# Other durations and a shared port in the build-time forecast of a two-layer fp32 backbone

## The chip, the cores and the metric

The kernel runs on one core of one Trainium2 chip. The metric is the time of one execution on the device in microseconds (us), as the median of several runs. In what follows PE is TensorE (and PEld its loading of stationary tiles), DVE is VectorE, ACT is ScalarE, POOL is GpSimd, and SP is SyncE, whose queue issues most transfers.

## The reference, cut to what matters

Two layers work on 512 latent tokens and 256 context tokens of width 1024, in fp32. Each layer has three token mixers side by side (multi-head latent attention, a bidirectional gated linear recurrence, HGRN2, and differential attention), fed by one input projection. Their outputs are merged by gates, and a SwiGLU block follows.

```python
for l in range(DEPTH):                                   # DEPTH = 2
    sh1, sc1, g1, sh2, sc2, g2 = split(silu(c) @ w_mod[l] + b_mod[l], 6)
    y_x, y_c = token_mixer(x * (1 + sc1) + sh1, ctx * (1 + csc1) + csh1, ...)
    x = post_norm(x, g1 * y_x, ln1_g[l], ln1_b[l])
    x = post_norm(x, g2 * swiglu(x * (1 + sc2) + sh2, w_ff1[l], w_ff2[l]), ...)
    # the context stream likewise, in layer 0 only
# token_mixer: y0 = latent attention, y1 = HGRN2, y2 = differential attention
m = sum(sigmoid(h @ w_gate[i] + b_gate[i]) * (y[i] @ w_branch[i]) for i in range(3))
y = m @ w_o
```

## The kernel before

**Products.** A weight block of 128 x 1024 is loaded (wr), cast to a rounded type (wh), and what the cast lost is subtracted out (wl = wr - wh). The activations are split in the same way (h, k, s or ac, in two tiles each). A product is then three matmuls: high by high, high by low, low by high (`mm3`, line 462). The accumulators are PSUM banks of 512 columns, named b; S names the pair of two-bank tiles. Every weight block is a `Job`, and `dstep` (line 394) emits the next few matmuls of the current job: six of them, then it gives its cost by `mmcost`. `do_conv` and `split_w` (lines 365 and 352) make wh and wl a job or two ahead, `pump` (line 332) issues the loads.

**Chains.** The attentions, the recurrence and the layer norms are written as generators of small steps, each of which waits for the one before: `mla`, `diff` and `hgrn` in this order, then the norms. In the recurrence (`hgrn`, line 1334) each of the four heads runs seven levels. A level has the products S of kc and QQ on PE (line 1406), an update of the key tile KK on POOL (line 1411), a copy kc of it by ACT for the next level, two updates of the query tile QQ and a masked copy out of S on DVE (lines 1424 and 1426). KK, QQ and TT are called k in the profile, since all come from one pool; kc, and everything else of one slab, is called s. Behind the last level come transposes of KK, the running states, the output products, a norm, and the store of y to DRAM (line 1503). The last merge reads y back (`yprep`, line 1525), and its eight products with `w_branch` can't begin without it. The eight products with `w_gate` ahead of them can.

**What sets the order.** Nothing does at run time but the five queues and the semaphores. The order within a queue is the order in which the build emits instructions. `weave` (line 433) runs a chain's generator; where the chain says `At(t)`, the time at which its next operands are due, it emits `dstep`s of products until PE's forecast time gets to t - 0.1. The forecast is the class `Clock` (line 110): for each instruction emitted it works out a start (its engine free, operands written, the output tile free) and a duration by engine, operation and columns, in `note` (line 188). Two choices read the forecast as well: `split_w` gives the cast to POOL rather than ACT where POOL is forecast to be over 1 us earlier (not within the recurrence), and `lo_eng` (line 360) gives the subtraction of certain jobs to DVE rather than POOL within the recurrence, where DVE is forecast to be free earlier than POOL plus 1 us. `pump` loads a block when its buffer is forecast to be free within 3 us of PE's time. Every instruction goes through the helper at line 106, so all rows of the profile have that line.

Of the kernel before, what the change touches and what calls it, by code (L numbers as in the profile page):

```python
# [10 lines left out]
F32 = mybir.dt.float32  # L11
# [28 lines left out]
def mmcost(n):  # L40
    return max(n, 250) * 0.000422

# [55 lines left out]
class Port:  # L98
    """an engine's queue, each instruction noted by the clock before it is emitted"""
    def __init__(self, clock, eng):  # L100
# [9 lines left out]
class Clock:  # L110
    """A coarse forecast, in us, of when each engine gets to what is put in its queue and when each tile is written.
    It only decides how many steps of the weight products are put between two steps of a latency-bound chain."""

    def __init__(self, nc):
        self.nc = nc
        self.at = dict(tensor=0.0, vector=0.0, scalar=0.0, gpsimd=0.0, sync=0.0)
        self.busy = []
        self.wrote, self.used, self.prev, self.rings = {}, {}, {}, {}
        for e in ("tensor", "vector", "scalar", "gpsimd", "sync"):
            setattr(self, e, Port(self, e))  # L120

    def ring(self, key, bufs, tile):
        """the tile takes the buffer of the one allocated bufs before it under the same tag"""
        r = self.rings.setdefault(key, [])
        name = tile.tensor.name
        r.append(name)
        if len(r) > bufs:
            self.prev[name] = r[-bufs - 1]
        return tile
# [35 lines left out]
    def next(self, key, bufs):  # L165
        """when a tile allocated now under this tag can be written"""
        r = self.rings.get(key, ())
        return self.whole(r[-bufs]) if len(r) >= bufs else 0.0

    def mark(self, log, ap, end, eng):  # L170
# [5 lines left out]
    def transfer(self, t, c):  # L176
        """the first free stretch of the DMA rings from t on"""
        for i, (a, b) in enumerate(self.busy):
            if a >= t + c:
                self.busy.insert(i, (t, t + c))  # L180
                break
            t = max(t, b)
        else:
            self.busy.append((t, t + c))
        self.busy = self.busy[-100:]
        return t + c

    def note(self, eng, op, a, k):
        outs = [a[0]] + ([k["accum_out"]] if "accum_out" in k else [])
        ins = [x for x in list(a[1:]) + list(k.values()) if hasattr(x, "tensor") and hasattr(x, "ap")]  # L190
        sizes = [x.free_size() for x in outs[:1] + ins]
        n = sizes[0] if eng == "tensor" else max(sizes[:3])
# [7 lines left out]
        if op == "dma_start":  # L200
            self.at[eng] = start + (0.53 if eng == "sync" else 1.1)
            end = self.transfer(start + 0.6, outs[0].size() * 4 / 360e3) + 1.4
        else:
            if eng == "tensor":
                slow = op == "transpose" or n < 250 or ins[0].dtype == F32
                c, lat = max(n * (0.00084 if slow else 0.000422), 0.03) * (2 if ins[0].dtype == F32 and op != "transpose" and n < 250 else 1), 0.2
            elif eng == "vector":
                c, lat = 0.065 + n * (0.00052 if op == "tensor_copy" else 0.00065 if op == "tensor_scalar" else 0.00105), 0.15
            elif eng == "scalar":
                c, lat = 0.09 + n * 0.00083 + (0.1 if len(outs) > 1 else 0.0), 0.15  # L210
            else:
                c = 0.13 + n * (0.00101 if op == "tensor_scalar" else 0.00212) + (0.3 if ALU.pow in a else 0.0)
                lat = 0.15
            self.at[eng] = start + c
# [7 lines left out]
class At:  # L222
    """go on when the products put in the queue reach this time"""
    def __init__(self, t):
# [17 lines left out]
class Kern:  # L242
# [144 lines left out]
    def ahead(self, i, n):  # L387
        """the end of the list of weights up to the n-th after the i-th that goes to the tensor engine"""
        while n and i + 1 < len(self.wjobs):
            i += 1  # L390
            n -= self.wjobs[i].conv is None
        return i + 1
# [106 lines left out]

    # ---------------------------------------------------------------- setup  # L500
    def setup(self):
# [20 lines left out]
    def setup_rows(self):  # L522
        """loads of the small parameters, as rows"""
        nc, I, cp = self.nc, self.I, self.cp
# [85 lines left out]

    # ---------------------------------------------------------------- adaLN modulation vectors
    def mod_block(self, l, blk, direct=False):
# [60 lines left out]
    def mod_block_v(self, l, blk):  # L673
        """as mod_block, the products and their sum over blocks of 128 inputs elementwise, the sum over partitions by ones"""
        nc, I = self.nc, self.I
# [81 lines left out]
    def affine(self, key, l, which, ln):  # L757
        """per-feature gain and offset of x -> x * (1 + sc) + sh, after the gain and offset of a layer norm if any"""
        nc = self.nc
# [12 lines left out]
    def mod_tile(self, key, t, xo, h):  # L772
        """h[:, :, tile t] = transpose(xo) * A + B, split in two parts"""
        hx = self.ln4()
# [33 lines left out]

    # ---------------------------------------------------------------- latent query/key front
    def b1_load(self, l, u, dma):  # L810
# [157 lines left out]

    # ---------------------------------------------------------------- combined input projection (rest)
    def win_jobs(self, l, names):  # L970
        """feature-major tiles of w_in, parked in DRAM"""
        nc = self.nc
# [21 lines left out]

    # ---------------------------------------------------------------- multi-head latent attention
    def mla(self, l):
# [134 lines left out]

    # ---------------------------------------------------------------- differential attention
    def diff(self, l):
# [194 lines left out]

    # ---------------------------------------------------------------- bidirectional gated recurrence
    def vw(self, t, off, dims):  # L1330
# [184 lines left out]

    # ---------------------------------------------------------------- gated merge
    def merge_jobs(self, l, br, seq):
# [66 lines left out]

    # ---------------------------------------------------------------- token-major output products
    def sweep_jobs(self, key, w, nk, tiles, lhs, use_s, needs=(), keep=2):
        """acc[t] = lhs(:, t)^T w; the last blocks of w are kept for a pass tile by tile, so that the tiles end one after the other"""
        nc = self.nc
# [60 lines left out]
    def ln_front(self, x1, r):  # L1649
        """x1 <- ALPHA * r + x1; the scale and offset of its normalization"""  # L1650
        nc = self.nc
# [72 lines left out]

    # ---------------------------------------------------------------- FFN
    def ff1_jobs(self, l):
# [267 lines left out]
```

## Time and profile before

| what | us |
|---|---|
| median of 3 runs | 3069.2 (3064.12 to 3072.55) |
| span of the profiled execution, which is its own time | 3064.3 |
| PE busy, in all | 2825.8 |
| DVE busy | 1628.7 |
| ACT busy | 1137.7 |
| POOL busy | 974.2 |
| layer 0: latent attention, from 172 to 408 | 236 |
| layer 0: differential attention, 408 to 652 | 244 |
| layer 0: recurrence, 652 to 946 | 294 |
| layer 1: the same three, 1899 to 2106, to 2303, to 2546 | 207, 197, 243 |

The span is the time from the first to the last instruction of the one execution that was profiled. Busy times of different engines overlap. A stage here is the stretch in which the chain of that mixer runs, with products of the weights between its steps; I set its ends by the first and last instructions of the chain. "Clock" below is the granted clock of TensorE as a share of 2.4 GHz; at 0.5 it is at its lower level, 1.2 GHz.

### The profile page before, as it was taken

What the parts mean: (1) busy time and instruction counts of PE and PEld (TensorE: products, weight loads), DVE (VectorE), ACT (ScalarE), POOL (GpSimd) and SP (SyncE); (2) the same over time, 40 slices, a digit from 0 to 9 for tenths busy, and PEclk for the clock granted to TensorE, in tenths of its full rate; (3) what the DMA queues carried; (4) which work ended last, traced back from release to release, by engine and by line L of the source; (5) the groups of instructions that cost most, each with busy time, mean ns of one, the idle gap of its engine ahead of it and who ended that gap; (6) DMA issues with size and microseconds to landing.
All of it is one profiled execution on the core that took longest, in us unless ns stands there. A gap on an engine that the chain in (4) does not pass through costs nothing. (4 is left out here: it accounts for less than half of the span.)

```text
span 3064.3 us, 39087 instructions
## 1 busy us (share of the span) xinstructions
PE 2825.8 (92%) x14899; PEld 2346.2 (77%) x14899; DVE 1628.7 (53%) x2413; ACT 1137.7 (37%) x2177; POOL 974.2 (32%) x688
## 2 busy tenths in 40 slices
PE   6999989998799997999999898999998899799997
PEld 3888866677688885888888677887776777688875
DVE  4455566657762038555543665445656762632235
ACT  4544434443332124344332445444444332322222
POOL 1333433334444434243320223333324555300002
PEclk8999999999999998999999999999999999899998
DMA  6423243343333354354443354324223343433331
GB/s 211 129 80 97 91 136 96 100 141 103 101 111 110 103 169 151 117 152 143 119 137 96 110 167 122 89 83 131 79 73 127 104 132 123 146 107 96 103 131 69
DMA packets 345523, 359.14 MB, mean 117 GB/s; under 512 B 31114, under 2 KB 263044, under 8 KB 345336
## 3 DMA queue, kind: packets, MB, share of 16 engines
q1 hardware_dynamic: 343144, 351.84, 37.0%
q10 hardware_dynamic: 1680, 4.42, 0.4%
q8 instruction: 117, 1.92, 0.3%
q14 instruction: 70, 0.57, 0.1%
q0 software_dynamic: 512, 0.39, 0.1%
HBM read 298.10 MB, written 58.49 MB: 116 GB/s over the span
## 5 line engine op out<-in xcount | busy, mean ns | idle before, releaser
L106 PE MATMUL b<-h,wh 128*128 128x512 f32 (+1 forms) x5152 | 1385.0, 358 | 32.2 <-ACT h L106 14.2
L106 PEld LDWEIGHTS b<-h,wh 128*128 128x128 f32 x5152 | 911.5, 193 | 168.3 <-ACT h L106 15.1
L106 PE MATMUL b<-h,wl 128*128 128x512 f32 (+1 forms) x2576 | 909.5, 353 | 0.0
L106 DVE TENSOR_TENSOR wl<-wr,wh 128x1024 fp32r<-128x1024 f32 (+1 forms) x253 | 373.0, 1478 | 458.3 <-ACT wh L106 457.3
L106 PEld LDWEIGHTS b<-h,wl 128*128 128x128 f32 x2576 | 496.6, 193 | 66.4 <-DVE wl L106 0.3
L106 ACT CAST wh<-wr 128x1024 fp32r<-128x1024 f32 (+1 forms) x298 | 295.0, 993 | 415.2 <-PE b L106 331.2
L106 POOL TENSOR_TENSOR sm<-sm,mhalf 128x1 f32<-128x1 f32 (+3 forms) x80 | 56.7, 709 | 1035.7 <-DVE sm L106 1035.7
L106 POOL TENSOR_TENSOR wl<-wr,wh 128x1024 fp32r<-128x1024 f32 (+1 forms) x131 | 285.5, 2179 | 222.4 <-ACT wh L106 199.9
L106 ACT ACTIVATE s<-S,sm 128x768 f32<-128x768 f32 (+1 forms) x170 | 135.2, 796 | 377.7 <-DVE sm L106 325.2
L106 POOL TENSOR_TENSOR ln<-ln,wr 128x512 f32<-128x512 f32 x84 | 119.5, 1423 | 222.9 <-issue 161.6
L106 PE MATMUL S<-wh,ac 128*128 128x512 f32 x512 | 173.8, 404 | 16.4 <-DVE ac L106 11.2
L106 PE MATMUL S<-k,s 128*128 128x128 f32 (+2 forms) x704 | 150.8, 336 | 37.8 <-DVE k L106 33.8
L106 DVE TENSOR_TENSOR k<-b,k 128x512 fp32r<-128x512 f32 (+1 forms) x136 | 85.0, 627 | 175.0 <-ACT k L106 174.7
L106 PE MATMUL S<-k,k 96*128 96x512 f32 (+2 forms) x576 | 153.0, 366 | 22.8 <-DVE k L106 11.8
L106 PE MATMUL b<-k,wh 128*128 128x512 f32 (+1 forms) x576 | 161.5, 368 | 10.5 <-ACT k L106 6.9
L106 DVE TENSOR_REDUCE sm<-S 128x1 f32<-128x768 f32 (+1 forms) x160 | 131.5, 839 | 70.1 <-PE S L106 70.0
L106 PEld LDWEIGHTS S<-k,s 128*128 128x128 f32 (+1 forms) x704 | 107.4, 207 | 76.8 <-issue 51.2
L106 PEld LDWEIGHTS S<-k,k 96*128 96x128 f32 (+1 forms) x576 | 103.5, 196 | 63.4 <-issue 16.9
L106 PE MATMUL b<-ident,s 128*128 128x128 f32 (+3 forms) x687 | 111.8, 276 | 42.5 <-DVE s L106 19.3
L106 POOL TENSOR_SCALAR wh<-wr 128x1024 fp32r<-128x1024 f32 (+1 forms) x86 | 88.7, 1036 | 188.5 <-PE b L106 179.3
L106 POOL TENSOR_TENSOR s<-s,s 128x512 f32<-128x512 f32 (+2 forms) x88 | 112.4, 1288 | 90.2 <-DVE s L106 45.6
L106 DVE TENSOR_TENSOR k<-s,k 96x768 fp32r<-96x768 f32 (+7 forms) x92 | 108.8, 1209 | 52.3 <-ACT k L106 48.3
(184 smaller groups left out, 4128.5 us busy)
## 6 DMA issues: line engine op xcount, KB each, us to landing
wr<-in_w_ff_dram SPq DMA_DIRECT2D x154, 512.0 KB
wr<-in_w_mod_dram SPq DMA_DIRECT2D x96, 512.0 KB
d<-s SPq DMA_DIRECT2D x88, 384.0 KB
wr<-in_w_in_dram SPq DMA_DIRECT2D x64, 512.0 KB
s<-d SPq DMA_DIRECT2D x80, 384.0 KB
wr<-in_w_gate_dram SPq DMA_DIRECT2D x48, 512.0 KB
wr<-in_w_branch_dram SPq DMA_DIRECT2D x48, 256.0 KB
wr<-in_w_o_dram SPq DMA_DIRECT2D x24, 512.0 KB
```

What stands on the lines that cost most here:

```text
L106: return getattr(getattr(self.clock.nc, self.eng), op)(*a, **k)
```

## The change

The class `Clock` and `mmcost` get other numbers, and the forecast gets one more rule. No instruction of the kernel is added or removed.

- A product costs 0.443 ns a column, at least 0.118 us, instead of 0.422 ns and at least 250 columns: 0.227 us instead of 0.216 for 512 columns, 0.118 instead of 0.108 for 256. Transposes and short fp32 matmuls have numbers of their own.
- On DVE the quick rates of a copy and of a tensor-scalar operation apply only if no operand is in PSUM.
- An ACT operation with a tensor as its scale costs 0.08 more; POOL's two rates change by a few per cent.
- `port`: a DVE operation that works on SBUF alone, and is a copy, a tensor-scalar operation or has two wide inputs, starts in the forecast only when no POOL operation is running, and a POOL operation only when no such DVE operation is. The last 24 stretches of each are kept.

Lines that hold only comments or docstrings are also gone in the new version; they are left out here.

```diff
@@ -38,7 +38,7 @@
 def mmcost(n):
-    return max(n, 250) * 0.000422
+    return max(n * 0.000443, 0.118)
...
@@ -108,19 +108,20 @@
         self.busy = []
+        self.held = dict(vector=[], gpsimd=[])
...
@@ -163,9 +164,19 @@
+    def port(self, other, start, c):
+
+        for a, b in self.held[other]:
+            if a <= start < b:
+                start = b
+        mine = self.held["vector" if other == "gpsimd" else "gpsimd"]
+        mine.append((start, start + c))
+        del mine[:-24]
+        return start
...
@@ -188,6 +199,7 @@
+        wide = [x for x in ins if x.free_size() > 1 or outs[0].free_size() == 1]
...
@@ -201,16 +213,32 @@
+            lat = 0.15
             if eng == "tensor":
-                slow = op == "transpose" or n < 250 or ins[0].dtype == F32
-                c, lat = max(n * (0.00084 if slow else 0.000422), 0.03) * (2 if ins[0].dtype == F32 and op != "transpose" and n < 250 else 1), 0.2
+                if op == "transpose":
+                    c = 0.109 if n > 64 else 0.062
+                elif ins[0].dtype == F32:
+                    c = 2 * max(n * 0.00084, 0.112)
+                else:
+                    c = max(n * 0.000443, 0.118)
+                lat = 0.2
             elif eng == "vector":
-                c, lat = 0.065 + n * (0.00052 if op == "tensor_copy" else 0.00065 if op == "tensor_scalar" else 0.00105), 0.15
+                flat = not any(x.space == bass.MemoryType.PSUM for x in outs + ins)
+                if op == "tensor_copy" and flat:
+                    c = 0.067 + n * 0.00052
+                elif op == "tensor_scalar" and flat:
+                    c = 0.067 + n * 0.00064
+                else:
+                    c = 0.067 + n * 0.00104 + (0.06 if op == "scalar_tensor_tensor" else 0.0)
+                if flat and (op in ("tensor_copy", "tensor_scalar") or len(wide) > 1):
+                    start = self.port("gpsimd", start, c)
             elif eng == "scalar":
-                c, lat = 0.09 + n * 0.00083 + (0.1 if len(outs) > 1 else 0.0), 0.15
+                c = 0.09 + n * 0.00083 + (0.1 if len(outs) > 1 else 0.0)
+                if hasattr(k.get("scale"), "tensor"):
+                    c += 0.08
             else:
-                c = 0.13 + n * (0.00101 if op == "tensor_scalar" else 0.00212) + (0.3 if ALU.pow in a else 0.0)
-                lat = 0.15
+                c = 0.13 + n * (0.00094 if op == "tensor_scalar" else 0.00219) + (0.3 if ALU.pow in a else 0.0)
+                start = self.port("vector", start, c)
             self.at[eng] = start + c
             end = start + c + lat
```

Since the forecast sets the order, the diff doesn't show what moves. In the order of PE, names are tiles with their number; `b` is a bank of products, `S` a level of the recurrence, `wh` and `wl` the halves of a weight block, `128x512` or `128x256` the columns, and `x2` two in a row.

Layer 0, recurrence, head 1, PE: the products ahead of its last level. Before:

```order
L106 MATMUL S_7319<-k_7074,s_7293 128x128 x6
L106 MATMUL b_7312<-k_6541,wh_7187 128x512 x2
L106 MATMUL b_7312<-k_6541,wl_7188 128x512
L106 MATMUL b_7312<-k_6546,wh_7187 128x512 x2
L106 MATMUL b_7312<-k_6546,wl_7188 128x512
L106 MATMUL S_7344<-k_7074,s_7327 128x128 x6
```

After, the same place:

```order
L106 MATMUL S_7330<-k_7031,s_7313 128x128 x6
L106 MATMUL b_7346<-k_6447,wh_7199 128x256 x2
L106 MATMUL b_7346<-k_6447,wl_7200 128x256
L106 MATMUL b_7346<-k_6452,wh_7199 128x256 x2
L106 MATMUL b_7346<-k_6452,wl_7200 128x256
L106 MATMUL b_7346<-k_6457,wh_7199 128x256 x2
L106 MATMUL b_7346<-k_6457,wl_7200 128x256
L106 MATMUL b_7346<-k_6462,wh_7199 128x256 x2
L106 MATMUL b_7346<-k_6462,wl_7200 128x256
```

Four products for the modulation vectors and twelve of 512 columns stand behind these, and only then the last level, S_7390. Where six products stood ahead of that level, there are 28.

Layer 1, recurrence, last head, PE: two of its last levels. Before:

```order
L106 MATMUL S_21514<-k_21209,s_21465 128x128 x4
L106 MATMUL b_21507<-k_20831,wh_21445 128x512 x2
L106 MATMUL b_21507<-k_20831,wl_21446 128x512
L106 MATMUL b_21507<-k_20836,wh_21445 128x512 x2
L106 MATMUL b_21507<-k_20836,wl_21446 128x512
L106 MATMUL S_21538<-k_21209,s_21520 128x128 x4
L106 MATMUL b_21554<-k_20821,wh_21480 128x512 x2
L106 MATMUL b_21554<-k_20821,wl_21481 128x512
L106 MATMUL b_21554<-k_20826,wh_21480 128x512 x2
L106 MATMUL b_21554<-k_20826,wl_21481 128x512
L106 MATMUL b_21554<-k_20831,wh_21480 128x512 x2
```

After, its last four levels and what follows them:

```order
L106 MATMUL S_21793<-k_21618,s_21780 128x128 x4
L106 MATMUL S_21805<-k_21618,s_21799 128x128 x4
L106 MATMUL S_21817<-k_21618,s_21811 128x128 x4
L106 MATMUL S_21829<-k_21618,s_21823 128x128 x4
L106 MATMUL b_21840<-ident,k_21617 128x128 x4
L106 MATMUL b_21846<-ident,k_21617 128x128
L106 MATMUL b_21850<-ident,k_21617 128x128 x4
L106 MATMUL b_21857<-ident,k_21617 128x128
L106 MATMUL b_21862<-s_21637,s_21839 128x128
```

Between these levels, and between them and the transposes (`ident`), no product stands any more; the products of this stretch have moved ahead, into the first three heads.

Layer 1, recurrence, first head, POOL: its queue over five levels (`k` by `k` or `s` is the update of KK). Before:

```order
L106 TENSOR_TENSOR k_19942<-k_19942,k_19944 128x384x2
L106 TENSOR_TENSOR wl_20053<-wr_19862,wh_20052 128x1024
L106 TENSOR_TENSOR k_19942<-k_19942,s_20018 128x192x2x2
L106 TENSOR_TENSOR k_19942<-k_19942,k_19944 128x96x2x4
L106 TENSOR_TENSOR wl_20109<-wr_19928,wh_20108 128x512
L106 TENSOR_TENSOR k_19942<-k_19942,s_20018 128x48x2x8
L106 TENSOR_TENSOR k_19942<-k_19942,k_19944 128x24x2x16
L106 TENSOR_TENSOR k_19942<-k_19942,s_20018 128x12x2x32
```

After:

```order
L106 TENSOR_TENSOR k_19982<-k_19982,k_19984 128x384x2
L106 TENSOR_TENSOR wl_20085<-wr_19919,wh_20084 128x512
L106 TENSOR_TENSOR k_19982<-k_19982,s_20060 128x192x2x2
L106 TENSOR_TENSOR k_19982<-k_19982,k_19984 128x96x2x4
L106 TENSOR_TENSOR wl_20164<-wr_20063,wh_20163 128x512
L106 TENSOR_TENSOR k_19982<-k_19982,s_20060 128x48x2x8
L106 TENSOR_TENSOR wl_20199<-wr_20095,wh_20198 128x1024
L106 TENSOR_TENSOR k_19982<-k_19982,k_19984 128x24x2x16
```

Subtractions (`wl`) stand between the updates at more of the levels than before.

## Rows read from the trace of the kernel before

**Rows 1.** The page's first lines: span; busy time, share, instructions of each engine.
```profile
span 3064.3 us, 39087 instructions
...
PE 2825.8 (92%) x14899; PEld 2346.2 (77%) x14899; DVE 1628.7 (53%) x2413; ACT 1137.7 (37%) x2177; POOL 974.2 (32%) x688
```

**Rows 2.** Windows by stage: stretch and length, busy of PE, PEld, DVE, ACT, POOL, clock, DMA, GB/s.
```profile
172.00:408.00 236.00, 225.03 (x1398) 196.90 (x1397) 127.65 (x240) 107.14 (x240) 87.82 (x75) 0.98 0.34 103
408.00:652.00 244.00, 224.76 (x1164) 170.68 (x1163) 159.48 (x298) 100.15 (x253) 79.50 (x64) 0.96 0.31 96
652.00:946.00 294.00, 258.30 (x1591) 221.85 (x1592) 204.87 (x269) 111.08 (x207) 121.41 (x63) 0.95 0.34 113
...
1899.00:2106.00 207.00, 200.52 (x1241) 179.56 (x1242) 96.80 (x179) 85.81 (x183) 77.24 (x60) 0.97 0.30 87
2106.00:2303.00 197.00, 190.08 (x946) 146.07 (x945) 123.84 (x214) 84.51 (x199) 59.30 (x45) 0.95 0.29 87
```

**Rows 3.** Waits of PE in 652 to 946: us in total, times, longest.
```profile
PE S L106 <- DVE k L106: 22.6, 11, 4.2
```

**Rows 4.** Timeline from 764: start, us, engine, operation, count, [idle before <- releaser].
```profile
764.08 1.87 POOL L106 TENSOR_TENSOR wl<-wr,wh 128x512 fp32r<-128x512 f32 x1 [3.02 <-ACT wh L106]
764.26 0.62 PE L106 MATMUL b<-h,wh 128*128 128x512 f32 x2
...
764.72 4.10 DVE L106 TENSOR_TENSOR k<-k,k 128x384 f32<-128x384 f32 x2
...
764.95 0.61 PE L106 MATMUL b<-h,wh 128*128 128x512 f32 x2
...
765.91 2.49 POOL L106 TENSOR_TENSOR k<-k,s 128x768 f32<-128x768 f32 x1
...
769.65 1.21 DVE L106 TENSOR_TENSOR wl<-wr,wh 128x1024 fp32r<-128x1024 f32 x1
...
797.08 1.03 DVE L106 TENSOR_TENSOR k<-k,k 128x384 f32<-128x384 f32 x2 [0.18 <-PE S L106]
```

**Rows 5.** Windows, after a wait of PE in the recurrence of layer 0.
```profile
892.43:896.10 3.67, 3.67 (x15) 3.48 (x16) 1.08 (x2) 0.00 (x0) 0.00 (x0) 0.54 0.43 128
```

**Rows 6.** Timeline of PE in and behind that stretch.
```profile
892.43 2.74 PE L106 MATMUL S<-k,s 128*128 128x128 f32 x12 [2.29 <-DVE k L106]
...
894.82 1.20 PE L106 MATMUL b<-h,wh 128*128 128x512 f32 x2
...
896.16 0.63 PE L106 MATMUL b<-h,wh 128*128 128x512 f32 x2
```

**Rows 7.** Windows of heads 0, 1 and 2 of layer 1's recurrence.
```profile
2320.00:2379.00 59.00, 55.99 (x299) 47.27 (x299) 45.17 (x62) 20.19 (x38) 31.16 (x18) 0.95 0.33 105
2379.00:2437.00 58.00, 49.16 (x258) 41.64 (x259) 37.75 (x59) 18.66 (x36) 30.38 (x19) 0.91 0.33 108
2437.00:2495.00 58.00, 53.75 (x282) 44.53 (x280) 43.04 (x62) 21.91 (x42) 27.09 (x20) 0.97 0.41 133
```

**Rows 8.** Timeline of the last head of layer 1's recurrence.
```profile
2514.29 1.05 PE L106 MATMUL S<-k,s 128*128 128x128 f32 x8
...
2518.27 1.57 POOL L106 TENSOR_TENSOR k<-k,k 128x768 f32<-128x768 f32 x1
...
2519.87 0.62 ACT L106 COPY s<-k 128x512 f32<-128x512 f32 x1 [7.35 <-POOL k L106]
...
2523.77 2.40 POOL L106 TENSOR_TENSOR wl<-wr,wh 128x1024 fp32r<-128x1024 f32 x1 [1.68 <-ACT wh L106]
...
2532.26 1.67 PE L106 MATMUL b<-ident,k 128*128 128x128 f32 x10 [1.32 <-POOL k L106]
...
2535.15 2.39 PE L106 MATMUL b<-s,s 128*128 128x128 f32 x20
...
2546.63 0.34 SPq L106 DMA_DIRECT2D d<-s  x1
...
2552.70 5.54 DVE L106 TENSOR_TENSOR k<-s,k 128x512 fp32r<-128x512 f32 x4 [6.10 <-ACT k L106]
```

## The prediction

> **What bounds the kernel now.** I read the busy shares first: TensorE (PE) is busy for 2825.8 of 3064.3 us [rows 1], and its list of matmuls is the same in both kernels, 14,367 in the program. So the span can only change by PE's idle time, 3064.3 - 2825.8 = 238.5 us, and by the time in which PE runs at the lower of its two clocks. Next I cut the span by stages and took length minus PE busy in each [rows 2]: latent attention of layer 0 (172 to 408) 11.0 idle, differential attention (408 to 652) 19.2, recurrence (652 to 946) 35.7; in layer 1 the two attentions 6.5 and 6.9. The recurrence of layer 1 is cut by heads [rows 7]: 3.0, 8.8 and 4.3 in heads 0 to 2. The rest of the idle time lies at the start, the layer norms and the end, where the change moves next to nothing.
>
> Then the waits by engine: in the recurrence of layer 0, 22.6 us of the 35.7 are the level's products (S) waiting for VectorE's update of a key or query tile k [rows 3]. The timeline shows why a step is late. Two query updates took 1.03 us where GpSimd did nothing and 4.10 where it worked through a subtraction and a key update; that key update took 2.49 us [rows 4], against 1.57 alone [rows 8]. The weave of the kernel before doesn't know of this: it puts as many weight products ahead of a level as cover the undisturbed steps. Those products run at 0.69 us for three of 512 columns, 0.23 each [rows 4], where its forecast has 0.216; the new one has 0.227.
>
> Idle time costs a second time. In the 3.67 us after one such wait the granted clock was 0.54, so most of it at 1.2 GHz [rows 5]; two products took 1.20 us there and 0.63 right behind it [rows 6]. A mean granted clock of 0.95 over 294 us [rows 2] is (1 - 0.95) x 2 x 294 = 29 us at 1.2 GHz; PE is busy in 88% of the stage, and half of that busy time is lost: about 13 us.
>
> **The change part by part.** All of it is forecast. Its effect is where weight products stand in PE's queue, and which engine makes the two halves of a weight tile. I priced PE's order, chain step by chain step, at 0.227 us for a product of 512 columns (half for 256), and followed the sum of what stands ahead of each step in the kernel after, minus before.
>
> 1. Layer 0, latent attention: the sum falls to -14 us. The chain there waits little (11.0 idle in 236), so less cover can open waits; but the chain's own slack is small, and the products aren't lost, only later. Bounds: -4 (a quicker chain) and +8 (half of the 14 exposed). I take +2, near the first row of the stage.
>
> 2. Layer 0, differential attention: a further swing to -20 us. In many tiles a group of products of 4 to 5 us moves from one side of the score products to the other. Bounds 0 and +15 (three such groups uncovered); the row of the stage has 19.2 idle, most of the cover being more than enough, so I stay near the lower end: +4.
>
> 3. Layer 0, recurrence: +20 us of products move into the heads, back to about 0 at the end, since 210 us of products that need nothing of it are left in both kernels: there is no shortage. About 14 of the 20 stand ahead of levels that waited. Idle -14; the lost clock goes with it, 13 x 14 / 35.7 = 5. Together -19. Bounds: 0 (the levels become late by as much as is put before them) and -40 (nearly all waits and the clock).
>
> 4. Layer 1, both attentions: the sum goes from -6 to +3. I take -2 of 13.4 idle; bounds -6 and +6.
>
> 5. Layer 1, recurrence, heads 0 to 2: 1.4 to 4 us of products a level become 4 to 11; +61 us by the start of head 3. A bare level costs GpSimd's update 1.57, ScalarE's copy 0.62 [rows 8] and some 0.2 of hand-over, 2.4 us; with VectorE and GpSimd in each other's way I allow twice that, still less than what stands before it. So all waits go: -(3.0 + 8.8 + 4.3) = -16. The clocks of 0.95, 0.91 and 0.97 are 5.9 + 10.4 + 3.5 = 19.8 us at 1.2 GHz [rows 7], at 91% busy a loss of 9, which goes too: -25.
>
> 6. The tail of that recurrence is the other side of 5. The products run out: in the kernel before 29.9 us of them stand after level 3 of the last head, after it 1.4. Four levels, the transposes, the states, the output products and the norm then run bare: 4 x 2.4, and from the transposes at 2532.26 to the store of y at 2546.63 14.4, of which the products between delayed at most 0.4 [rows 8]: 24.0 us. PE's own work in it is 4 x 1.05 + 1.67 + 2.39 [rows 8] and 28 more matmuls at the 0.12 of the last row, 3.4: 11.7. Idle 12.3. Then what is left (65.3 us of products, in the kernel before 100.7 of which 35.4 need no y) needs y back from DRAM: from the store at 2546.63 to VectorE's split at 2552.70, and 0.8 for it, 6.9 us [rows 8], which the kernel before covers. 12.3 + 6.9, less the 1.3 that PE waits there now: +18. Bounds +10 (loads quicker, the chain at 2 us a level) and +30 (levels at the pace of the disturbed pair in rows 4, three us more each).
>
> 7. The weight splits: in the program 14 subtractions move from VectorE to GpSimd, and 11 casts from GpSimd to ScalarE. In the recurrences it is 7 (layer 0) and 15 (layer 1) more subtractions on GpSimd. One takes 2.40 us there [rows 8] and 1.21 on VectorE alone [rows 4]. It stands between two key updates on GpSimd's queue, and the next key update and its copy are queued behind it. In layer 1 4 to 11 us of products cover that, and I take 0 there; in layer 0 it is in the bound 0 of term 3. If the cover is gone, the port is held 1.19 us longer for each, 7 x 1.19 = 8 and 15 x 1.19 = 18.
>
> The layer norms and the entry have their queue order within some products of before: 0. **Sum:** 2 + 4 - 19 - 2 - 25 + 18 = -22, a span of 3042. The median of the three runs shown is 3069.2, 4.9 above the profiled span, so the time is 3047.
>
> On term 7 a rule speaks against the change. In rows 4 two updates that take 1.03 alone took 4.10, 3.07 more: the subtraction on GpSimd ran on for 1.23 after their start, and the key update alone would be 1.57, 2.80 together. The Trainium skill ("SBUF — State Buffer", section "SBUF: two separate sides") states that VectorE and GpSimd share a port pair as an exclusive lock: who starts first holds it for the whole instruction, and the other fully blocks. The trace agrees within 0.3 us. By that rule each moved subtraction would block VectorE for the whole 2.40, and the sum would be -22 + 26 = +4 if none is covered; rival B below has that mechanism.
>
> **The rivals.**
> A, no difference: the heads give back idle time but not clock, and the attention of layer 0 loses what I only allowed as a bound: 2 + 12 - 14 - 2 - 16 + 18 = 0, 3069. For it: the gain and the tail of layer 1 are nearly equal, and the -14 and -20 of terms 1 and 2 are of the size of what term 3 gains. Against it: low clocks stand beside waits [rows 5].
> B, slower: GpSimd holds the port for the moved subtractions while VectorE's updates of the chain wait. The place is the levels of both recurrences, the price 1.19 us for each of 22, and the waits that I let go in layer 0 stay: 2 + 4 + 8 - 2 - 25 + 18 + 18 = +23, 3092. With the gain of term 3 gone the sum is -3, so it becomes slower by over 9 us from some 10 of the 22 that meet the chain uncovered. For it: rows 4. Against it: the same forecast puts more products ahead of each level.
> C, much faster: every wait of the recurrences in layer 0 goes with its clock (-40), and the tail costs 10: -40 - 25 + 10 = -55, 3014. For it: the new duration of a product, 0.227, is the trace's 0.23. Against: the forecast still has no queue of waits as long as the trace's 4.2 us [rows 3].
> That the change doesn't do what it says would show as a key update that the forecast has at 1.81 us and the trace at 1.57 [rows 8]: it overfills, which costs nothing before the tail, and is in A.
>
> **How the numbers follow.** Forecast 0.42, A 0.25, B 0.21, C 0.12. About 0.3%, 9 us, is what can be told from no change. Faster 0.42 + 0.12 = 0.54, same 0.25, slower 0.21. The likeliest time is 3047, its own range 3033 to 3060 (terms 3 and 6 between their nearer bounds). With half of C and half of B left out, the range is 3018 to 3090.
>
> **What would show it.** Right: in heads 0 to 2 of layer 1 PE idles under 4 us in all, at a clock near 1.0; the last head has some 12 us of idle, then 6 to 7 of waiting for y's reload; S waits for k in layer 0's recurrence for about 10 us instead of 22.6. Wrong: waits of S for VectorE as before or longer, beside subtractions on GpSimd (B); new waits in 172 to 652 of over 15 us (A); a last head without idle time, which would mean that the products didn't run out.

## The result, and the profile after

The changed kernel takes 3099.33 us (median of 4 runs, 3091.8 to 3111.87) against 3070.88 before (median of 4, 3064.12 to 3074.84). The ratio is 1.010, with a 95% interval of 1.008 to 1.012: slower by 1%, where I had forecast faster by 0.7%, and outside my range. The page of the profiled execution, its span and the busy times:

```profile
span 3099.0 us, 39079 instructions
...
PE 2834.2 (91%) x14899; PEld 2353.3 (76%) x14899; DVE 1644.0 (53%) x2399; ACT 1148.5 (37%) x2188; POOL 997.5 (32%) x691
```

Against [rows 1] the span is 34.7 us longer. PE's idle time, span minus busy, went from 238.5 to 264.8, +26.3; PE is busy for 8.4 more with the same matmuls. It was busy at the lower clock for 184.4 us instead of 174.3 (PE's busy time within the stretches whose granted clock is 0.5); two products took 1.20 us there for 0.63 [rows 6], so I estimate that half of these 10 us, some 5 of the 8.4, is the clock. The waits of PE over the whole run (in total, times, longest), the kernel before first:

```profile
PE S L106 <- DVE k L106: 45.5, 29, 4.2
...
PE b L106 <- ACT s L106: 12.5, 9, 2.7
...
PE b L106 <- ACT k L106: 10.4, 2, 6.9
```

and after:

```profile
PE b L106 <- ACT s L106: 32.4, 14, 12.8
...
PE S L106 <- DVE k L106: 26.7, 21, 3.6
PE b L106 <- ACT k L106: 18.1, 2, 12.2
```

The waits of S for VectorE's k fell from 45.5 to 26.7. That is the wait that the change was made of and that the forecast spoke of, and it went the right way by 18.8 us. But PE's banks b wait 19.9 us more for ScalarE's s and 7.7 more for its k.

I then cut both spans at the same instructions of the chains. "Products" is what the two orders differ by in that stage, at 0.227 us for 512 columns; "rest" is the difference of the lengths less these, so it is what the stage itself gained or lost. These are two single profiles; how far such lengths spread with one and the same order is told in the last section.

| stage | before, us | after, us | products | rest | predicted |
|---|---|---|---|---|---|
| start | 172.0 | 173.8 | 0 | +1.7 | 0 |
| layer 0, latent attention | 239.8 | 233.3 | -13.0 | +6.5 | +2 |
| layer 0, differential attention | 242.5 | 248.2 | +0.7 | +5.0 | +4 |
| layer 0, recurrence and merges | 508.5 | 524.9 | +10.8 | +5.5 | -19 |
| first norm, FFN | 651.1 | 659.3 | +1.3 | +6.9 | 0 |
| second norm | 85.2 | 87.6 | 0 | +2.4 | 0 |
| layer 1, both attentions | 423.8 | 421.6 | 0 | -2.2 | -2 |
| layer 1, recurrence and merge | 333.2 | 336.7 | 0 | +3.5 | -7 |
| the end | 408.2 | 413.5 | 0 | +5.2 | 0 |

**Layer 0's recurrence.** The waits of PE from 655 to 965 in the kernel after, which answer to [rows 3]:

```profile
PE b L106 <- ACT s L106: 14.6, 4, 12.8
PE S L106 <- DVE k L106: 13.8, 8, 3.6
PE b L106 <- DVE s L106: 11.0, 10, 2.4
```

S for k fell from 22.6 to 13.8, but one wait of 12.8 is new. The timeline around it (start, us, engine, operation, [idle before <- releaser]):

```profile
679.45 2.42 SPq L106 DMA_DIRECT2D s<-d  x5
...
682.82 2.69 SPq L106 DMA_DIRECT2D s<-d  x4
...
689.17 0.83 ACT L106 CAST k<-s 128x768 fp32r<-128x768 f32 x1 [9.62 <-DMA s<-d]
...
695.17 3.04 ACT L106 ACTIVATE k<-s 128x768 f32<-128x768 f32 x4
...
700.15 0.57 ACT L106 COPY s<-b 128x512 f32<-128x512 f32 x1
...
700.30 0.69 PE L106 MATMUL b<-ident,s 128*128 128x128 f32 x2 [12.79 <-ACT s L106]
```

At 679.45 SyncE issues the recurrence's five rows, at 682.82 the reload of y for the first merge, which is queued behind them. Four casts of that y stand in ScalarE's queue *ahead* of the first head's sigmoids. ScalarE waits 9.62 us for the transfer, the sigmoids begin at 695.17 only, the copy out of the transposes comes at 700.15, and PE stands for 12.79 us. In the kernel before, the four sigmoids stand ahead of the casts, and PE waits 2.13 us at these transposes:

```profile
673.52 3.07 ACT L106 ACTIVATE k<-s 128x768 f32<-128x768 f32 x4 [2.55 <-DMA s<-d]
...
679.83 0.44 PE L106 MATMUL b<-ident,s 128*128 128x128 f32 x2 [2.13 <-ACT s L106]
...
680.88 1.81 ACT L106 CAST k<-s 128x768 fp32r<-128x768 f32 x2 [0.17 <-DMA s<-d]
```

The two orders of ScalarE's queue differ there by where a `Job` ends. Between the recurrence's loads and its first head the build emits 3 us of products (`yield 3.0`). In the new order a job with a product of `w_gate` begins within them, and with it `ytry` emits the reload; in the old order a job that was begun earlier fills them.

**Layer 1's recurrence.** Windows of heads 0 to 3, which answer to [rows 7]:

```profile
2348.80:2408.00 59.20, 58.75 (x311) 50.06 (x309) 39.81 (x55) 22.14 (x42) 37.00 (x22) 0.98 0.34 110
2408.00:2485.00 77.00, 72.07 (x356) 59.17 (x356) 46.97 (x63) 26.71 (x48) 46.08 (x27) 0.96 0.46 146
2485.00:2555.00 70.00, 68.30 (x356) 57.12 (x356) 51.13 (x57) 24.15 (x43) 48.69 (x26) 1.00 0.44 134
2555.00:2603.00 48.00, 37.76 (x203) 33.36 (x204) 31.22 (x50) 16.02 (x33) 26.80 (x17) 0.86 0.07 23
```

Idle time in heads 0 to 2 is 0.5 + 4.9 + 1.7 = 7.1 us (16.1 before), the last head has 10.2 at a clock of 0.86. Behind it:

```profile
2602.66 0.63 PE L106 MATMUL b<-ident,s 128*128 128x128 f32 x4 [3.43 <-DVE s L106]
...
2604.11 0.34 SPq L106 DMA_DIRECT2D d<-s  x1
...
2608.58 0.62 ACT L106 CAST k<-s 128x512 fp32r<-128x512 f32 x1 [7.60 <-DMA s<-d]
...
2609.25 1.52 PE L106 MATMUL b<-k,wh 128*128 128x512 f32 x2 [5.96 <-ACT k L106]
```

The products have run out; the store of y goes out at 2604.11, and PE waits 5.96 us for the first split. So the tail came near the prediction: 10.2 and 5.96 for 12.3 and 6.9. Not predicted was the same thing ahead of head 0, where the first merge of layer 1 reloads its y:

```profile
2337.38 3.37 SPq L106 DMA_DIRECT2D s<-d  x4
2345.08 2.58 ACT L106 CAST k<-s 128x512 fp32r<-128x512 f32 x4 [10.26 <-DMA s<-d]
...
2345.75 1.52 PE L106 MATMUL b<-k,wh 128*128 128x512 f32 x2 [12.16 <-ACT k L106]
```

12.16 us; at the same place the kernel before waits 6.9, the longest of its waits of b for ScalarE's k above.

### The profile page after: what moved, and what is told of

It reads as the page before. It is cut to its first block, busy times and chain, and to the rows that moved or that the text cites. A ratio compares the mean times of both kernels' runs of the same rounds, so it can differ in the third digit from the quotient of the medians.

```text
span 3099.0 us, 39079 instructions
## 1 busy us (share of the span) xinstructions
PE 2834.2 (91%) x14899; PEld 2353.3 (76%) x14899; DVE 1644.0 (53%) x2399; ACT 1148.5 (37%) x2188; POOL 997.5 (32%) x691
## 5 line engine op out<-in xcount | busy, mean ns | idle before, releaser
L106 PE MATMUL b<-h,wh 128*128 128x512 f32 (+1 forms) x5152 | 1381.4, 357 | 40.9 <-ACT h L106 16.7
L106 DVE TENSOR_TENSOR wl<-wr,wh 128x1024 fp32r<-128x1024 f32 (+1 forms) x239 | 350.0, 1467 | 458.1 <-ACT wh L106 454.7
L106 ACT CAST wh<-wr 128x1024 fp32r<-128x1024 f32 (+1 forms) x309 | 304.5, 990 | 414.7 <-PE b L106 343.2
L106 POOL TENSOR_TENSOR wl<-wr,wh 128x1024 fp32r<-128x1024 f32 (+1 forms) x145 | 320.7, 2212 | 273.5 <-ACT wh L106 252.9
L106 PE MATMUL S<-wh,ac 128*128 128x512 f32 x512 | 173.6, 404 | 17.8 <-DVE ac L106 12.8
L106 DVE TENSOR_TENSOR k<-b,k 128x512 fp32r<-128x512 f32 (+1 forms) x136 | 85.2, 627 | 166.9 <-ACT k L106 166.5
L106 PE MATMUL S<-k,s 128*128 128x128 f32 (+2 forms) x704 | 148.2, 331 | 21.8 <-DVE k L106 16.1
L106 PEld LDWEIGHTS S<-k,s 128*128 128x128 f32 (+1 forms) x704 | 105.8, 201 | 59.1 <-issue 35.5
L106 PEld LDWEIGHTS b<-ident,s 128*128 128x128 f32 (+3 forms) x687 | 82.7, 145 | 89.3 <-ACT s L106 35.9
```

Of the source, the lines that this page charges most:

```text
L106: return getattr(getattr(self.clock.nc, self.eng), op)(*a, **k)
```

## Experiments: which part of the change

Three kernels take one part of the change each, into the kernel before. The expectations below speak of three theories of the loss. Theory 1: the blocked queue of ScalarE, that is, the reload of y ahead of the first head's sigmoids. Theory 2: the port rule. Theory 3: the dearer product of PE, which makes the weave put fewer products ahead of a step.

p_pe: PE's costs alone.

```diff
 def mmcost(n):
-    return max(n, 250) * 0.000422
+    return max(n * 0.000443, 0.118)
...
             if eng == "tensor":
-                slow = op == "transpose" or n < 250 or ins[0].dtype == F32
...
+                if op == "transpose":
+                    c = 0.109 if n > 64 else 0.062
```

> The kernel before with the new costs of PE's instructions alone (mmcost and the durations on the tensor engine). Theory 3 (a dearer product makes the weave put too few products ahead of the steps of the attentions): most of the loss is here, 1.007 or more. Theory 2 (the port): within 0.3% of before. Theory 1: this order too has the reload of y ahead of the first head's sigmoids, so about 10 us slower than before, 1.003, by that block alone.

Measured: 3092.07 us, ratio 1.008 (1.006 to 1.011). Two of its waits:

```profile
PE S L106 <- DVE k L106: 50.7, 40, 5.3
PE b L106 <- ACT s L106: 32.1, 15, 13.2
```

The time is what theory 3 expected. S waits for k *more* than before, 50.7, and the wait of 13.2 for ScalarE is the block. A dearer product means that fewer of them are needed to bring the forecast to the time of the next step: 116 us in layer 0's latent attention where before has 130, and the rest of that stage is +6.4.

p_dur: the durations of VectorE, ScalarE and GpSimd alone.

```diff
-                c, lat = 0.065 + n * (0.00052 if op == "tensor_copy" else ...
+                if op == "tensor_copy" and flat:
+                    c = 0.067 + n * 0.00052
```

> The kernel before with the new durations of VectorE, ScalarE and GpSimd alone, without the port and with PE's costs as before. In its order the reload of y stands behind the first head's sigmoids, as before, and the products in layer 1's heads are near those of before (27, 27, 40 and 40 us). All three theories expect it within 0.3% of before; another result would mean that a cause is missing.

Measured: 3093.34, 1.008 (1.005 to 1.011), against every theory.

```profile
PE S L106 <- DVE k L106: 48.7, 38, 3.2
...
PE b L106 <- ACT k L106: 23.4, 3, 11.6
```

S for k is no better, and PE waits 23.4 for the splits of y: 11.2 in layer 0 (a product that needs y stands in PE's own queue there, ahead of the chain) and 11.6 in layer 1.

p_port: the port alone.

```diff
+                flat = not any(x.space == bass.MemoryType.PSUM for x in outs + ins)
+                if flat and (op in ("tensor_copy", "tensor_scalar") or len(wide) > 1):
+                    start = self.port("gpsimd", start, c)
...
+                start = self.port("vector", start, c)
```

> The kernel before with the shared port in the forecast alone, all durations as before. Its order puts 42, 50 and 52 us of products into heads 0 to 2 of layer 1's recurrence (26, 23 and 35 before) and leaves 16 for the last head, as the kernel after does. Theory 2: most of the loss is here, 3095 or more (1.008). Theory 1: 3080 (1.003), the block of ScalarE's queue, which this order has too. Theory 3: within 0.3% of before.

Measured: 3065.49, 0.999 (0.998 to 1.000). Theory 2 is wrong, the port isn't the loss:

```profile
PE b L106 <- ACT k L106: 30.2, 3, 12.8
...
PE S L106 <- DVE k L106: 18.7, 18, 3.5
```

It more than halves the waits of S for k, from 45.5 to 18.7, and pays some three quarters of that back in waits for the split of y (30.2 in three places, 10.4 in two before). Its order starves the last head of layer 1 exactly as the kernel after does (16 us of products), and yet that stage is 5.5 us *better* than before.

## Experiments: the reload of y

a_fix: the kernel after, the reload not before the first head's copies.

```diff
-            if "y" not in st and f"y{l}_{br}" in self.done and ...
+            if not self.prep and "y" not in st and f"y{l}_{br}" in self.done and ...
```

> The kernel after, but the reload and split of y for the first merge may not be emitted until the first head of layer 0's recurrence has its sigmoids and copies in ScalarE's queue. Theory 1 (one blocked queue): the wait of 12.8 us of PE for ScalarE at the head's transposes falls to about 2, as in the kernel before, and the time falls by about 10 us, from 3099 to some 3089 (1.006 of before). Theories 2 and 3 (the cost is in how the forecast shares out the products, by the port or by the dearer product): the waits come back elsewhere and the time stays within 3 us of 3099.

Measured: 3091.52, 1.006 (1.003 to 1.009). The wait of 12.8 is 1.8, the gain about 8 by the medians, as theory 1 said, though the two intervals overlap. In the profiles layer 0's recurrence with its merges is the stage whose order changed, and it takes 512.4 us instead of 524.9, 12.5 less. Over half of the loss of the whole run is still there.

b_early: the kernel before, the reload put ahead of the sigmoids.

```diff
         self.inhg = True
         loads(0)
+        if l == 0:
+            self.ytry[l, 0]()
```

> The kernel before, with the one thing put in that the kernel after does at 652 us: the reload of y for the first merge is emitted at the start of layer 0's recurrence, ahead of the first head's sigmoids in ScalarE's queue. From the attentions on nothing else moves but some 10 us of products within that recurrence. Theory 1 (the blocked queue): PE waits 10 to 13 us at the head's transposes, and the time is 10 us above before, 1.003. Rival (the block is hidden by products, and the 12.8 us that the profile of after shows there are given back later): within 3 us of before.

Measured: 3070.86, 1.001 (0.999 to 1.002). The block is there:

```profile
680.35 0.83 ACT L106 CAST k<-s 128x768 fp32r<-128x768 f32 x1 [11.23 <-DMA s<-d]
...
686.17 1.12 PE L106 MATMUL b<-ident,s 128*128 128x128 f32 x4 [8.17 <-ACT s L106]
...
690.92 0.69 PE L106 MATMUL b<-ident,s 128*128 128x128 f32 x2 [3.64 <-ACT s L106]
```

PE stands for 8.17 + 3.64 us, and the time is the same. PE's waits in the four heads sum to 35.5 us against 34.1 before: later ones went away (2.90, 3.37 and 3.47 us in the first two heads of before have no counterpart). PE's busy time at the lower clock in that stage fell from 28.6 to 18.2 us, too. So theory 1 in its simple form, a stall of 12 us is 10 us of time, is wrong, and the rival holds: with this forecast the stall was given back.

b_y, a_y, a_y0, port_y, pe_y, dur_y: the reload taken apart. The loads are issued as before; the casts and subtractions are emitted only when the forecast has the loads landed, and a product that needs y isn't offered before that.

```diff
+    def ysplits(self, force=False):
+        if self.yq and (force or self.ck.ready(*self.yq[0][0]()) <= max(self.ck.at["scalar"], self.ck.at["tensor"])):
+            self.yq.pop(0)[1]()
...
     def dstep(self):
+        self.ysplits()
...
+                yield Need(f"yr{l}_{br}")
```

> The kernel before, with the reload of y taken apart: the loads are issued at once, the split on ScalarE and VectorE and the products that need y only when the forecast has the loads landed. Before had no such block in layer 0 except 9 us of ScalarE near 890. Theory 1: equal to before or up to 5 us faster (0.998 to 1.000).

> The kernel after with the same taking apart of the reload. Theory 1 with theory 3: the block's 10 us go, as in a_fix (1.006), and what PE's dearer products cost in the attention of layer 0 and in the layer norms stays: 1.004 to 1.006. If the port is a gain and the block the only loss, 0.997.

> The kernel after with the reload of y taken apart in layer 0's merges only; in layer 1 it is emitted as in the kernel after. Taken apart everywhere it gave 0.998 of before against 1.010. If the two places of layer 1 (12.2 us ahead of the first head, 6.0 us behind the last) count beside the one in layer 0 (12.8), this ends between: some 13 us above a_y, 3074 (1.002). If layer 0's place alone is the cause, it equals a_y, 3061 (0.998).

> The port alone (p_port) with the same taking apart of the reload. p_port has one wait of 12.8 us of PE for ScalarE's split of y, and is at 0.999 of before. Theory 1: that wait goes, 10 to 12 us less, 3054 (0.995). If the loss of p_port's order lay in layer 1's tail rather than here, it would stay at 0.999.

> PE's new costs alone (p_pe, 1.008) with the reload of y taken apart. If the reload is what turns other orders into slower ones, the 13.2 us of layer 0's recurrence go, and it is at 1.003 to 1.004. If a dearer product by itself opens waits (theory 3), it stays within 3 us of 1.008.

> The new durations of VectorE, ScalarE and GpSimd alone (p_dur, 1.008) with the reload of y taken apart. p_dur waits 15.7 us for the split of y in layer 0 and 11.6 in layer 1. By the reload theory these go: 3070 or less (1.000 or below). If the loss is in the durations themselves, it stays at 1.008.

| base | as it is | reload taken apart |
|---|---|---|
| before | 1 | 1.001 (1.000 to 1.003) |
| after | 1.010 (1.008 to 1.012) | 0.998 (0.996 to 0.999) |
| after, layer 0 only | | 0.999 (0.997 to 1.001) |
| port alone | 0.999 (0.998 to 1.000) | 0.999 (0.997 to 1.000) |
| PE's costs alone | 1.008 (1.006 to 1.011) | 1.007 (1.004 to 1.009) |
| other durations alone | 1.008 (1.005 to 1.011) | 1.005 (1.003 to 1.006) |

a_y comes out near the second of its readings, 0.997. a_y0, 3070, lies between its 3061 and 3074. pe_y stays within 3 us of p_pe, as theory 3 said, and port_y stays at 0.999. b_y misses its range by 0.001, and dur_y (3087.94) met neither of its readings.

On the kernel after the edit is worth 38 us (3099.33 to 3061.01), most of it in layer 0 (3070.05). On the others of this table it is worth little or nothing. In the kernel after it does more than take the stall away. The same stage in a_fix and in a_y0 (length, busy of PE, PEld, DVE, ACT, POOL, clock, DMA, GB/s):

```profile
665.00:980.00 315.00, 285.75 (x1748) 247.11 (x1748) 203.17 (x268) 117.19 (x212) 141.76 (x74) 0.96 0.36 118
```

```profile
660.00:968.00 308.00, 290.11 (x1833) 252.83 (x1833) 216.54 (x280) 121.50 (x224) 145.47 (x78) 0.99 0.39 126
```

Same forecast, both without the block. In a_fix PE idles 29.3 of 315 us at a clock of 0.96, in a_y0 17.9 of 308 at 0.99. In a_fix ScalarE still stands 5.54 us for the reload of the second merge, in the last head; in a_y0 for none. The larger part is in the levels: S waits 11.7 us for k in that stage of a_fix, 0.4 in a_y0, and as little in a_y, from 664 to 963:

```profile
PE S L106 <- DVE k L106: 0.4, 1, 0.4
```

How the taking apart does away with these waits was not traced. Nor are the 38 us all the price of the new place: mix and mport below, whose reload in layer 0 stands behind the sigmoids, gain 17 to 19 us by the same edit.

What a blocked queue costs differs from kernel to kernel: 12.5 us of its stage in the kernel after, nothing in b_early. In pe_y the wait of 13.2 is gone, and layer 0's recurrence with its merges is 3.5 us shorter than in p_pe, but layer 1's is 13.1 longer, in single profiles. port_y and dur_y don't decide it, since the stall only changed its form there: PE stands 8.5 us for the recurrence's own loads in port_y, where it stood 12.8 for y in p_port, and 6.5 + 5.7 us in dur_y for 11.2 + 4.5 in p_dur. Why the same stall costs so differently isn't shown.

## Experiments: the new forecast in the recurrences alone

mix_y and mix: all of the new numbers while a recurrence is emitted, the old ones elsewhere, with and without the reload taken apart. mport_y and mport: the port alone, while a recurrence is emitted, all durations as before.

```diff
-                start = self.port("vector", start, c)
+                if self.hg:
+                    start = self.port("vector", start, c)
...
-        self.inhg = True
+        self.inhg = ck.hg = True
```

> The new numbers and the port within the two recurrences only, the old forecast everywhere else, the reload of y taken apart. If the new forecast is right for the recurrences (a_y: 23 us less there in layer 0 than before with equal products) and costs in the attention of layer 0 and in the norms (5 to 12 us each by stage), this beats all others: 3040 to 3050 (0.991 to 0.994). If the gain in the recurrences is bound to the orders of the stages ahead, it is near a_y, 0.998.

> mix_y without the taking apart of y's reload: the whole new forecast within the recurrences, the old one elsewhere, the reload as before. In this order the reload in layer 0 stands behind the sigmoids. If the reload counts by its place alone, it costs some 5 to 10 us against mix_y (3044), from layer 1's two places: 3050 to 3055. If taking it apart is needed for the gain at all, 3065 or more.

> The kernel before, the shared port put into its forecast within the two recurrences alone; all durations and PE's costs as before, the reload of y as before. If the port is the part of the change that is right and the numbers do the harm, this is clearly faster than before: S waits for k as in p_port (18.7 us in all, 45.5 before), and y's reload in layer 0 stays behind the sigmoids: 3050 to 3055 (0.995). If the gain of mix_y came from the new numbers, it is within 0.2% of before.

> mport with the reload of y taken apart. If the numbers add nothing, it equals mix_y within 5 us, 3040 to 3050; if the new numbers within the recurrences are worth something beside the port, it is over 5 us slower than mix_y.

| | as it is | reload taken apart |
|---|---|---|
| new numbers and port, recurrences only | 3063.35, 0.998 (0.996 to 0.999) | 3043.93, 0.991 (0.988 to 0.993) |
| port alone, recurrences only | 3045.80, 0.992 (0.990 to 0.993) | 3028.64, 0.988 (0.985 to 0.990) |

The best is mport_y, 1.2% faster than before and 2.3% faster than the kernel after. Its page, its waits of S for k, and the window of layer 0's recurrence:

```profile
span 3026.7 us, 39079 instructions
...
PE 2806.7 (93%) x14899; PEld 2332.2 (77%) x14899; DVE 1650.2 (55%) x2402; ACT 1142.9 (38%) x2187; POOL 1000.4 (33%) x689
```

```profile
650.00:945.00 295.00, 282.94 (x1797) 245.34 (x1796) 207.31 (x273) 116.31 (x217) 151.65 (x79) 0.99 0.38 127
```

```profile
PE S L106 <- DVE k L106: 16.2, 15, 2.1
```

PE idles 220.0 us (238.5 before), S waits 16.2 for k (45.5), and in layer 0's recurrence 12 us of 295 are idle at a clock of 0.99, where [rows 2] has 35.7 of 294 at 0.95. The rest of that stage, cut as in the table above, is -34.2 us. In mport it is -26.2, which is all of the 25 us that mport gains.

Of the expectations mix_y's held. mix, 3063, lies between its two readings. mport is better than its 3050 to 3055, although S still waits 29.9 us for k and not 18.7. mport_y is faster than either of its readings: neither allowed for new durations that cost time. In the recurrences they cost 17.6 us as it is, both kernels measured together; with the reload taken apart 9 us by the ratios and 15 by the medians, from two sessions whose intervals overlap.

So the port, in the recurrences, is the part of the change that is right. Its place matters: in the whole forecast it is worth 0.1% at most, 0.999 in both columns of the first table. There 23 us more of products than before are spent ahead of layer 0's recurrence, in the attentions, and the rest of that stage is -3.1 where mport has -26.2; no run shows that this is why. One thing holds for all kernels: in the ten that have the port in their forecast S waits 10.7 to 30.1 us in all for k, in the seven that don't 45.4 to 55.6. Two rivals are untested: a forecast that only makes the updates of k longer, without a lock, might put the same products there; and no neutral change of the numbers was run that would tell how much any new order moves the time, when p_pe and p_dur each moved it by 0.8%.

## Why the prediction was wrong

**The sum failed in term 3** (-19 predicted, +5.5 measured) and in its "0" for norms and ends (+16 with the start). The mechanism of term 3 is there in part: S waits 8.8 us less for k, where I had 14 less idle time. The clock that was to come back with it did not: PE was busy at the lower clock for 28.6 us of the stage before and 28.3 after, where I had 5 us back. And a wait of 12.8 us is new. Without it (a_fix) the stage's rest is -6.9, with the reload taken apart (a_y) -23.4. What I left out is the DMA and the queue behind it. I looked at PE's order and at GpSimd's; of ScalarE's I counted the casts. That the four casts of y stand ahead of the sigmoids could be read from the two orders, and what such a reload can take from the place near 898 of the trace before, where ScalarE waits 9.30 us for that of the next merge. I priced a reload in term 6 alone.

**Term 1** was too low: +6.5 for +2, and it repeats: 6.4 in p_pe, 5.7 in a_y, against -1.6 in p_port and 0.5 in p_dur. So it goes with PE's dearer products, and my upper bound of 8 held it. But it is less the open waits that I had in mind than the clock. PE's idle time there is 11.0 us before and 11.6, 10.9 and 11.1 in p_pe, a_fix and a_y (14.7 in after); its busy time at the lower clock rose from 10.2 to 17.3, 19.4 and 19.4 (12.8 in after). Half of that rise is 3.6 to 4.6 us. I had priced no clock there.

**Term 2**, +5.0 for +4, looks right in size by luck: after, a_fix, a_y and a_y0 have the same orders up to 655 us, and their rests are 5.0, 15.7, 12.4 and 15.6. By the means of the last section's table the rest is some +9.6, within my bounds of 0 and 15.

**Terms 5 and 6**: the heads lost 9 us of idle time for the 16 I expected, and 7.1 are left where I had named under 4. PE was busy there at the lower clock for 8.7 us instead of 18.3, some 5 us gained for the 9 I expected. The tail has 10.2 and 5.96 for 12.3 and 6.9; that its clock falls to 0.86 I had left out. The signs were right, the gain about half. The net came out at +3.5 for -7, with 12.16 for 6.9 at the reload ahead of head 0, which I hadn't looked at.

**Norms and ends**, 0 predicted: +6.9 in the first norm and FFN, seen in after (6.9), a_fix (8.9) and a_y (7.5), and in none of the parts alone (0.8, 0.8 and 1.4). In the kernel after, 4.7 of it is idle time. A subtraction on VectorE in the first norm takes 3.37 us there beside GpSimd's 5.96 us pair of updates, and PE waits 3.10 for it; before, PE's waits for a subtraction there are 0.39 and 1.33. This explains 1 to 2 of the 7, the rest was not traced. At the end (+5.2) PE idles 3.0 us more and is busy at the lower clock for 14.5 us instead of 8.8, of which difference half is 2.9; by the last section's table about 3 of the 5.2 repeat.

**The rivals.** B gave the time, 3092 for 3099, by luck and not by its mechanism: waits of S for k fell, where B needs them to stay, and the kernels with the port alone, with 140 to 144 subtractions on GpSimd (131 before, 145 after), aren't slower. Of A one half holds: the attention of layer 0 lost 11.5 us by the stage table, near A's 14; the gain in the recurrences that should have paid for it didn't come. C's sum left out terms 1, 2 and 4, +4 together, which would not have helped it. The Trainium skill's rule of the exclusive lock ("SBUF — State Buffer", section "SBUF: two separate sides") I had weighed as a reason against. In the runs a forecast that is taught such a lock, and nothing else, in the two recurrences is 0.8% faster (mport).

**What stays open.** Why the stall of b_early is given back in full and that of the kernel after isn't; I only see that the later waits and the time at the lower clock shrink. Why p_dur, whose products in the heads are near those of before, loses some 17 us in layer 0's recurrence, of which 15.7 is the wait for y, while b_early loses nothing with 11.8. And of the kernel after's 28 us the stall is some 8 (a_fix); how the others are made up is known by stage, and only in part by cause.

## What to carry to other kernels

When a build-time forecast or a cost table sets the order, compare *every* queue at the stage borders, and look first for instructions that wait for a transfer and have moved ahead of others on the same queue; PE stood 12 to 13 us for them here, and it takes a run to see whether that is paid (some 8 us, a_fix) or given back (b_early). Numbers that are nearer to the trace don't make a better order by themselves: a dearer filler means less of it (p_pe). Put a new rule of a forecast in alone, and first only where its wait is seen in the trace: here it was worth 0.8% there and 0.1% at most everywhere.

## What was unexpected of the hardware

The same queue orders ran through layer 0's differential attention in 248.2, 258.9 and 255.6 us in three kernels (after, a_fix, a_y), with PE idle for 20.8, 26.5 and 22.9 and busy at the lower clock for 30.4, 39.7 and 40.9. Idle time and clock both differ, with nothing changed in the program up to there. Other stages repeat far better. The lengths in us, one profile each, of kernels in which PE, VectorE, ScalarE and GpSimd all have the same order in that stage:

| stage | order of before | order of after |
|---|---|---|
| layer 0, latent attention | 238.9 to 240.3, 7 kernels | 232.3 to 233.3, 4 kernels |
| layer 0, differential attention | 242.4 to 249.3, mean 245.1, 7 | 248.2 to 258.9, mean 255.4, 4 |
| first norm, FFN | 650.0 to 652.1, 7 | 659.3 to 661.4, 4 |
| the end | 408.2 to 412.3, mean 410.3, 7 | 412.6 to 413.5, mean 413.2, 6 |

In layer 0's recurrence with its merges, a_y and a_y0 have the same order and take 495.9 and 492.5.

So a difference of one stage between two single profiles may be worth nothing below some 10 us in one stage, and be sure at 2 us in another; the medians of whole runs, and waits that repeat in several kernels, carry the argument here.
